# A hybrid of linear mixers and attention on one core: the first block's levels in PSUM pairs of their own, its third product in the product banks, and another order of the output product

## The chip, the cores and the metric

The kernel runs on one core of a Trainium2 chip. The metric is the device time of one execution in microseconds (us); lower is better.

## What is computed

The input x is 256 positions of 1024 numbers in float32. Two layers of a first block are followed by two layers of a second block; the change touches the first block only. In words of the reference, cut to what matters:

```python
def first_block(x, w_in, w_out, ...):
    for l in range(2):
        h = rms_norm(x, pre_mix_g[l])
        z = h @ w_in[l]                       # 1024 x 3256
        (a_q, a_f, a_i, a_g, b_q, b_k, b_v, b_code, b_g,
         c_q, c_kv, c_kr, d_q, d_k, d_v, d_beta, d_a, d_z) = split_columns(z)
        o_a = hgrn2_mixer(a_q, a_f, a_i, a_g, ...)
        o_b = gla_mixer(b_q, b_k, b_v, b_code, b_g, ...)
        o_c = mla_mixer(c_q, c_kv, c_kr, ...)
        o_d = gdn_mixer(d_q, d_k, d_v, d_beta, d_a, d_z, ...)
        mix = concatenate([o_a, o_b, o_c, o_d]) @ w_out[l]
        x = x + rms_norm(mix, post_mix_g[l])
        x = x + rms_norm(conv_glu_ffn(rms_norm(x, pre_ffn_g[l]), ...), post_ffn_g[l])
```

Each mixer gives 256 of the 1024 columns, in 4 heads of 64. a and b are gated linear attentions: for each pair of positions i >= j, the sum over the key's columns of q[i] k[j] exp(b[i] - b[j]), with b the running sum of the log gates, times v[j]. c is softmax attention with a low-rank query and key. d is the gated delta rule in chunks of 64, which needs the solution of a unit triangular system per chunk and head.

## The kernel before

**Products.** A weight comes from HBM in float32 (one DMA on the queue of SyncE, called SP below, per unit: L298) and is split on the chip into a high part by ScalarE (L308) and a low part by VectorE, now and then GpSimd (L311). A product of x and w is then three matmuls (`mm3`, L337 to L339: high x high, high x low, low x high), so the 48 matmuls of c's product (416 columns, two tiles of 128 positions, 8 blocks of the inner dimension) or the 96 of the output product (two tiles, two halves of 512 columns, 8 blocks of 128 rows of w_out) are counted with that three in them.

**PSUM.** Eight banks are four pairs, called acc, pd, pc and pa. A mixer's helper tiles come from `pt` (L198), which takes the mixer's pair from the table `BANKS` (L118). d has pd, c has pc, and a and b both have pa. Products without a bank of their own take the next of the rotation acc, acc, pa, pa (`acc`, L186); at c's product this rotation gives one bank of acc and one of pa. `first_banks` (L191) hands out both banks of a pair instead and moves the rotation on by the same two steps. The output product uses the banks of acc and pc.

**The mixers** (`first_layer`, L1293) are written as generators, planned in the order d, b, a, c. The levels of a and b are the function `gla` (L676). For each of 8 distances s it writes a decay table E (subtractions on VectorE, L711, and GpSimd, Exp on ScalarE), multiplies it with the queries on VectorE (L717, two rows per level) and with the keys on GpSimd (L721), takes eight matmuls into a bank of the mixer's pair (L735; L727 for the first level) and copies what the mask selects into the attention table A on VectorE (L744, two rows per level). L688 and L689 make the start of A, L752 and L753 apply it to the values, and `head_norm` (L581) with the transposes of L398 puts the result into mT, the input of the output product.

d's triangular system is solved in two parts. The 16 x 16 blocks on the diagonal go through DRAM (scr) into the tile d_Z and are inverted on VectorE by a recursion: seven pairs L1127, L1128, then L1130, L1131, L1132 and L1133, each needing the one before. The result goes out to DRAM (scv, L1134) and back as d_V (L1144). Then TensorE goes on, with steps on ScalarE and VectorE between: transposes (L1147), L1170, L1185, L1191, then the merging of blocks (L1162, L1178, L1191), and the recurrence over chunks (L1199 to L1233).

**What sets the order.** The program is written in the order of the generators, but each engine's order is made by the Tile framework's scheduler, which plays the program through a timeline of its own and starts what is ready. A bank, a buffer or a place in the plan of the weights (`ORDER1`, L28, is the order in which the eight blocks of w_out are loaded, split and multiplied; 0 and 1 are a's rows, 2 and 3 b's, 4 and 5 c's, 6 and 7 d's) therefore moves instructions on all engines. On the chip each engine runs its instructions in that order, one after the other, and waits where an input is not there yet.

Of the kernel before, what the change touches and what calls it, by code (L numbers as in the profile page):

```python
# [24 lines left out]
FF2 = 4096  # L25
EPS = 1e-6
NEG = -1e30
ORDER1 = (6, 7, 4, 5, 0, 1, 2, 3)  # L28
ORDER2 = (0, 1, 4, 5, 2, 3, 6, 7)
LEVELS = (32, 16, 8, 4, 2, 1)  # L30
WMAX = 1024
# [83 lines left out]
RUN2 = (0, 1, 0, 2, 1, 3, 0, 2, 3)  # L115
STAG = {"d": "d", "m": "d", "c": "c", "b": "c", "a": "a", "e": "e", "e2": "e"}

BANKS = {"m": ("pd", "pa"), "d": ("pd", "pd"), "c": ("pc", "pc"), "a": ("pa", "pa"), "b": ("pa", "pa"), "e": ("pa", "pa"), "e2": ("acc", "acc")}  # L118
NX = "N"
ACCS = ("acc", "acc", "pa", "pa")  # L120
NBANK = {"acc": 2, "pd": 2, "pc": 2, "pa": 2}
# [7 lines left out]
class K:  # L129
# [68 lines left out]
    def pt(self):  # L198
        self.turn = not self.turn
        return self.bank(BANKS[self.g][self.turn])  # L200

# [673 lines left out]
    def mixer_c(self, l, xT):  # L875
        nc, a = self.nc, self.a
# [8 lines left out]
        gn = self.z([128, 384], "c_gn")  # L885
        for ap, o, n in ((a["mla_q_norm_g"][l], 0, 256), (a["mla_kv_norm_g"][l], 256, 128)):
            nc.sync.dma_start(gn[:, o:o + n], bass.AP(tensor=ap.tensor, offset=ap.offset, ap=[[0, 128], [1, n]]))
        pz = self.tm(xT, (("c", l), 2, 416))
        kT = [self.z([96, 2, 256], "c_kT") for _ in range(2)]
        cT = [self.z([128, 256], "c_cT") for _ in range(3)]  # L890
        qT, V = [None] * 2, [None] * 2
# [345 lines left out]
    def plan_first(self, l, nxt):  # L1237
# [6 lines left out]
        for mixer in PLAN1:  # L1244
            for key, nk, c, n in blocks[mixer]:
                self.plan((key, l), w, D, nk, c, n)
        for kk in ORDER1:
            self.plan(("out", l, kk), a["w_out"][l, kk * 128:kk * 128 + 128], 128, 1, 0, D)
# [61 lines left out]
    def first_layer(self, l, last):  # L1310
# [9 lines left out]
        g2 = self.gains(a["post_mix_g"][l])  # L1320
        accs = self.big_out(self.mT, ("out", l), ORDER1)
        xT = self.norms((accs, g2, False), self.gains(a["pre_ffn_g"][l]))
# [455 lines left out]
```

## Time and profile before

| what | value |
|---|---|
| median of three runs | 1547.57 us (1544.92 to 1551.36) |
| the profiled execution's own time | 1551.53 us |
| its span on the core | 1549.4 us |
| mean granted clock of TensorE | 0.98 of full speed |
| TensorE busy | 1475.8 us, 95% |
| VectorE busy | 1002.3 us, 65% |
| ScalarE busy | 825.3 us, 53% |
| GpSimd busy | 280.1 us, 18% |
| DMA | 152 GB/s over the span |

The span is the time from the first instruction to the last on the core. The mixers of layer 0 lie at about 60 to 206 us of it, those of layer 1 at about 450 to 604; the rest are the FFNs and the second block. PE is TensorE, PEld its loading of weights, DVE VectorE, ACT ScalarE, POOL GpSimd, SP the queue of DMA issues. A matmul's time in the rows is longer than the distance to the next, since matmuls overlap in the pipeline.

### The profile page before, as it was taken

Reading aid. Unit: us, or ns where it says so; the run is one execution under the profiler, and the core shown is the slowest. Engines: PE = TensorE matmul, PEld = TensorE weight load, DVE = VectorE, ACT = ScalarE, POOL = GpSimd, SP = SyncE. Lnnn points to the kernel's source line nnn. Section 1 sums busy time; section 2 is a strip of 40 time slices with the busy share of each in tenths; the row PEclk is TensorE's granted clock in tenths of the full one; section 3 lists DMA queues with packets and bytes.
Section 4 is the critical chain, followed back from the end, with each engine's and each line's share of the span. In section 5 each row is a group of like instructions: output and inputs, shape, how many; then the busy total and the mean of one; then the engine's idle time right before and its main releaser. Section 6 shows DMA issues by size and latency. Waiting matters only on the chain.

```text
span 1549.4 us, 24775 instructions
## 1 busy us (share of the span) xinstructions
PE 1475.8 (95%) x9491; PEld 1319.9 (85%) x9491; DVE 1002.3 (65%) x1741; ACT 825.3 (53%) x1435; POOL 280.1 (18%) x360
## 2 busy tenths in 40 slices
PE   7988999999998899999999999999999999999998
PEld 6967789999896787999978888899977888899996
DVE  5896667656698665656576875554566695654455
ACT  5634456545565344544555674555554575555553
POOL 1453320000244232000033122000015231100010
PEclk9997999999999789999999999999999999999999
DMA  7532155656453223566646343556554543465563
GB/s 233 152 109 84 55 160 182 190 183 199 140 157 112 77 71 110 182 186 190 184 142 192 104 139 116 179 188 190 190 184 135 166 124 110 130 190 186 189 195 109
DMA packets 165379, 236.80 MB, mean 153 GB/s; under 512 B 16052, under 2 KB 127246, under 8 KB 165262
## 3 DMA queue, kind: packets, MB, share of 16 engines
q1 hardware_dynamic: 165262, 235.24, 49.1%
q8 instruction: 74, 1.21, 0.3%
q14 instruction: 43, 0.35, 0.1%
HBM read 232.45 MB, written 2.76 MB: 152 GB/s over the span
## 4 chain that ended last, share of the span: by engine, by line
PE 79%; DVE 11%; ACT 4%; DMA 4%; issue 1%; POOL 1%; SPq 0%; ACTq 0%; DVEq 0%
PE acc L337 7%; PE acc L338 7%; PE acc L339 7%; PE pa L337 7%; PE pa L339 7%; PE pa L338 7%; PE pc L337 5%; PE pc L339 5%; PE pc L338 5%; PE pd L339 4%; PE pd L338 4%; PE pd L337 4%; DVE wl L311 2%; DVE gl_r L717 2%; ACT wh L308 1%
## 5 line engine op out<-in xcount | busy, mean ns | idle before, releaser
L311 DVE TENSOR_TENSOR wl<-raw,wh 128x1024 fp32r<-128x1024 f32 (+4 forms) x424 | 484.3, 1151 | 364.0 <-ACT wh L308 362.8
L308 ACT ACTIVATE wh<-raw 128x1024 fp32r<-128x1024 f32 (+4 forms) x420 | 433.1, 1035 | 410.3 <-PE pd L338 100.1
L311 POOL TENSOR_TENSOR wl<-raw,wh 128x1024 fp32r<-128x1024 f32 (+1 forms) x26 | 61.6, 2370 | 641.9 <-ACT wh L308 641.6
L339 PE MATMUL pa<-xTh,wl 128*128 128x256 f32 x512 | 145.6, 284 | 0.0
L337 PE MATMUL pa<-xTh,wh 128*128 128x256 f32 x512 | 145.5, 284 | 0.0
L338 PE MATMUL pa<-xTl,wh 128*128 128x256 f32 x512 | 145.1, 283 | 0.0
L339 PE MATMUL pd<-xTh,wl 128*128 128x256 f32 x432 | 122.4, 283 | 0.5 <-DVE wl L311 0.5
L337 PE MATMUL pd<-xTh,wh 128*128 128x256 f32 x432 | 122.3, 283 | 0.0
L338 PE MATMUL pd<-xTl,wh 128*128 128x256 f32 x432 | 122.2, 283 | 0.0
L337 PEld LDWEIGHTS pa<-xTh,wh 128*128 128x128 f32 x512 | 98.2, 192 | 0.3
L338 PEld LDWEIGHTS pa<-xTl,wh 128*128 128x128 f32 x512 | 98.2, 192 | 0.3
L339 PEld LDWEIGHTS pa<-xTh,wl 128*128 128x128 f32 x512 | 98.1, 192 | 0.2
L337 PEld LDWEIGHTS pd<-xTh,wh 128*128 128x128 f32 x432 | 82.8, 192 | 0.9
L338 PEld LDWEIGHTS pd<-xTl,wh 128*128 128x128 f32 x432 | 82.8, 192 | 0.9
L339 PEld LDWEIGHTS pd<-xTh,wl 128*128 128x128 f32 x432 | 82.8, 192 | 0.8 <-DVE wl L311 0.8
L338 PE MATMUL acc<-wl,f_h 128*128 128x512 f32 x200 | 78.4, 392 | 0.0
L338 PE MATMUL pc<-wl,f_h 128*128 128x512 f32 x200 | 77.8, 389 | 0.0
L339 PE MATMUL pc<-wh,f_l 128*128 128x512 f32 x200 | 77.5, 389 | 0.0
L339 PE MATMUL acc<-wh,f_l 128*128 128x512 f32 x200 | 77.2, 389 | 0.0
L337 PE MATMUL acc<-wh,xTh 128*128 128x512 f32 (+4 forms) x200 | 71.3, 360 | 1.4 <-ACT xTh L494 1.1
L337 PE MATMUL pc<-wh,f_h 128*128 128x512 f32 x200 | 71.3, 389 | 0.0
L337 PE MATMUL acc<-wh,f_h 128*128 128x512 f32 x200 | 71.3, 392 | 0.0
(635 smaller groups left out, 3815.5 us busy)
## 6 DMA issues: line engine op xcount, KB each, us to landing
raw<-in_w_in_dram SPq DMA_DIRECT2D x84, 512.0 KB, 3.8
raw<-in_w_mlp_up_dram SPq DMA_DIRECT2D x64, 512.0 KB, 3.7
raw<-in_w_mlp_down_dram SPq DMA_DIRECT2D x64, 512.0 KB, 3.5
raw<-in_ffn_w_gate_dram SPq DMA_DIRECT2D x44, 512.0 KB, 3.6
raw<-in_ffn_w_up_dram SPq DMA_DIRECT2D x44, 512.0 KB, 3.5
raw<-in_ffn_w_down_dram SPq DMA_DIRECT2D x44, 512.0 KB, 3.6
raw<-in_w_out_dram SPq DMA_DIRECT2D x32, 512.0 KB, 3.6
raw<-in_w_ple_gate_dram SPq DMA_DIRECT2D x16, 512.0 KB, 3.4
```

The source lines that it names most:

```text
L308: nc.scalar.activation(h[:, p], raw[:, p], AF.Copy)
L311: e.tensor_tensor(l[:, p], raw[:, p], h[:, p].bitcast(F), OP.subtract)
L337: t.matmul(out, ah, bh, start=first, stop=False, skip_group_check=True)
L338: t.matmul(out, ah, bl, start=False, stop=False, skip_group_check=True)
L339: t.matmul(out, al, bh, start=False, stop=last, skip_group_check=True)
L717: nc.vector.tensor_tensor(R[:, j].rearrange("p h (b s) -> p h b s", s=s), ev[:, ft[j], :, 1][:, None].to_broadcast([128, 2, 128 // s, s]), ...
```

## The change

The diff is whole; it has three parts.

```diff
-ORDER1 = (6, 7, 4, 5, 0, 1, 2, 3)
+ORDER1 = (2, 3, 0, 1, 6, 7, 4, 5)
...
-BANKS = {"m": ("pd", "pa"), "d": ("pd", "pd"), "c": ("pc", "pc"), "a": ("pa", "pa"), "b": ("pa", "pa"), "e": ("pa", "pa"), "e2": ("acc", "acc")}
+BANKS = {"m": ("pd", "pa"), "d": ("pd", "pd"), "c": ("pc", "pc"), "a": ("pa", "pa"), "b": ("pc", "pc"), "e": ("pa", "pa"), "e2": ("acc", "acc")}
...
-        pz = self.tm(xT, (("c", l), 2, 416))
+        pz = self.tm(xT, (("c", l), 2, 416), outs=self.first_banks("acc"))
```

The blocks of w_out now come in the order b, a, d, c. Mixer b takes its helper tiles from the pair pc, which c uses too, and a keeps pa for itself. c's product goes into the two banks of acc. Nothing is computed in another way, and the number of instructions that compute stays as it was. Outside the mixer stages of the first block's two layers, the order of the engines is unchanged.

On VectorE the last steps of d's recursion in layer 0, from the sixth of the seven pairs on. Before:

```order
L1127 TENSOR_TENSOR d_tmp<-d_Z,d_Y 64x72
L1128 TENSOR_REDUCE d_Y<-d_tmp 64x2x6
L587 TENSOR_REDUCE hn_ssq<-hn_sq 128x4
L1127 TENSOR_TENSOR d_tmp<-d_Z,d_Y 64x98
L1128 TENSOR_REDUCE d_Y<-d_tmp 64x2x7
L1130 TENSOR_TENSOR d_tmp<-d_Y,d_Z 64x512
L1131 TENSOR_REDUCE d_U<-d_tmp 64x64
L590 TENSOR_TENSOR hn_y<-pa,rs 128x256
L1132 TENSOR_TENSOR d_tmp<-d_U,d_Y 64x512
L592 TENSOR_TENSOR hn_o<-hn_y,a_g 128x256
L1133 TENSOR_REDUCE d_Y<-d_tmp 64x8x8
```

With the change, the last four steps; both rows of the sixth and of the seventh pair stand ahead of these, with other rows between them:

```order
L717 TENSOR_TENSOR gl_r<-gl_e,gl_q 128x256 x2
L711 TENSOR_TENSOR gl_e<-a_b 128x256
L1130 TENSOR_TENSOR d_tmp<-d_Y,d_Z 64x512
L311 TENSOR_TENSOR wl<-raw,wh 128x1024
L587 TENSOR_REDUCE hn_ssq<-hn_sq 128x4
L1131 TENSOR_REDUCE d_U<-d_tmp 64x64
L717 TENSOR_TENSOR gl_r<-gl_e,gl_q 128x256 x2
L744 COPY_PREDICATED gl_a<-cu,pa 128x64x4 x2
L1132 TENSOR_TENSOR d_tmp<-d_U,d_Y 64x512
L590 TENSOR_TENSOR hn_y<-pc,rs 128x256
L744 COPY_PREDICATED gl_a<-cu,pa 128x128x2 x2
L1133 TENSOR_REDUCE d_Y<-d_tmp 64x8x8
```

The levels of a from the third on, which stood behind L1133 before, now stand between the steps of the recursion, all but the last two L744. In all, 34 rows newly stand ahead of L1133 in layer 0: seven L311, ten L717, ten L744, five L711 and two L689. In layer 1 they are these and two more L744, two L587, two L590, one L592 and one L401.

On TensorE around L1147, the first matmuls that need d_V, in layer 0. Before (three matmuls of c's product in a row are the three of one `mm3`):

```order
L753 MATMUL pa<-a_v,gl_a 128x64
L1147 MATMUL pd<-cf,d_V 128x128 x8
L1170 MATMUL pd<-d_T,d_MT 128x64 x8
L398 MATMUL pa<-cf,hn_o 128x128 x2
L337 MATMUL pa<-wh,xTh 128x416
L338 MATMUL pa<-wl,xTh 128x416
L339 MATMUL pa<-wh,xTl 128x416
L337 MATMUL pa<-wh,xTh 128x416
```

With the change:

```order
L753 MATMUL pc<-a_v,gl_a 128x64
L753 MATMUL pa<-a_v,gl_a 128x64 x4
L1147 MATMUL pd<-cf,d_V 128x128 x8
L1170 MATMUL pd<-d_T,d_MT 128x64 x4
L398 MATMUL pc<-cf,hn_o 128x128 x2
L1170 MATMUL pd<-d_T,d_MT 128x64 x4
L912 MATMUL pc<-cf,c_cn 128x128 x3
L913 MATMUL pc<-cf,c_cn 96x128
L337 MATMUL acc<-wh,mTh 128x512
L338 MATMUL acc<-wl,mTh 128x512
L339 MATMUL acc<-wh,mTl 128x512
```

Before, 30 of the 48 matmuls of c's product and all levels of a stood behind L1147; now c's product is complete and a's levels are done before it, and six matmuls of the output product (into acc) follow it. Of the output product's 96 matmuls, 18 stood ahead of d's last L398 and 78 behind it; now 27 stand between L1147 and d's last L1233, and 69 behind. In layer 1, nine stand ahead of L1147, 41 between and 46 behind.

On SP around d's store and loads in layer 0, before:

```order
L1122 DMA d_Z<-scr 64x16x16
L881 DMA c_wuq<-in_mla_w_uq_dram 128x384 x2
L884 DMA c_wkv<-in_mla_w_ukv_dram 128x512
L887 DMA c_gn<-in_mla_q_norm_g_dram 128x256
L887 DMA c_gn<-in_mla_kv_norm_g_dram 128x128
L1134 DMA scv<-d_Y 64x16x16
L1144 DMA d_V<-scv 128x4x128 x2
L298 DMA raw<-in_w_out_dram 128x1024 x6
```

With the change:

```order
L1122 DMA d_Z<-scr 64x16x16
L298 DMA raw<-in_w_out_dram 128x1024 x2
L881 DMA c_wuq<-in_mla_w_uq_dram 128x384
L298 DMA raw<-in_w_out_dram 128x1024
L881 DMA c_wuq<-in_mla_w_uq_dram 128x384
L884 DMA c_wkv<-in_mla_w_ukv_dram 128x512
L887 DMA c_gn<-in_mla_q_norm_g_dram 128x256
L887 DMA c_gn<-in_mla_kv_norm_g_dram 128x128
L298 DMA raw<-in_w_out_dram 128x1024
L298 DMA raw<-in_ffn_w_gate_dram 128x4x256
L1134 DMA scv<-d_Y 64x16x16
L1144 DMA d_V<-scv 128x4x128 x2
```

Before, two loads of w_out were ahead of the store of scv, and six and the first of the FFN behind it; now all eight and that one are ahead.

## Rows read from the trace of the kernel before

**Rows 1.** Stretch, its length, busy PE, PEld, DVE, ACT, POOL, clock, DMA share, GB/s
```profile
88.04:124.01 35.97, 24.84 (x130) 20.61 (x129) 29.79 (x77) 6.88 (x16) 14.11 (x26) 0.83 0.32 89
124.01:182.66 58.65, 55.55 (x422) 48.64 (x423) 38.18 (x84) 30.09 (x84) 19.73 (x36) 0.93 0.26 83
182.66:206.29 23.63, 23.63 (x120) 19.31 (x120) 12.23 (x24) 10.05 (x19) 8.31 (x7) 1.00 0.39 122
485.58:516.34 30.76, 17.19 (x89) 14.79 (x88) 24.94 (x65) 4.22 (x11) 11.19 (x20) 0.75 0.27 75
516.34:578.50 62.16, 58.55 (x422) 51.46 (x423) 39.28 (x90) 30.63 (x86) 20.18 (x37) 0.88 0.26 82
578.50:604.22 25.72, 25.62 (x120) 21.23 (x121) 12.58 (x25) 10.02 (x19) 8.31 (x7) 0.92 0.37 109
```

**Rows 2.** Busy time of VectorE to the recursion's end, layers 0 and 1
```profile
88.04:118.76 30.72, 28.94 (x75) 0.89 0.31 87
485.58:510.50 24.92, 23.45 (x62) 0.81 0.26 75
```

**Rows 3.** Timeline, layer 0: start, us, engine line op out<-in [idle before <-releaser]
```profile
118.09 0.67 DVE L1133 TENSOR_REDUCE d_Y<-d_tmp 64x64 f32<-64x512 f32 x1
...
118.84 0.59 SPq L1134 DMA_DIRECT2D scv<-d_Y  x1
...
124.01 1.11 PE L1147 MATMUL pd<-cf,d_V 128*128 128x128 f32 x4 [1.73 <-DMA d_V<-scv]
```

**Rows 4.** VectorE, 88 to 119: group xcount | busy us, mean ns | idle before
```profile
L717 DVE TENSOR_TENSOR gl_r<-gl_e,gl_q 128x256 f32<-128x256 f32 x22 | 10.2, 513 | 0.0
```

**Rows 5.** VectorE's groups from 130 to 206 us
```profile
L311 DVE TENSOR_TENSOR wl<-raw,wh 128x1024 fp32r<-128x1024 f32 x8 | 9.6, 1220 | 4.0 <-ACT wh L308 4.0
L717 DVE TENSOR_TENSOR gl_r<-gl_e,gl_q 128x256 f32<-128x256 f32 x10 | 7.4, 777 | 0.3 <-ACT gl_e L713 0.3
L744 DVE COPY_PREDICATED gl_a<-cu,pa 128x256 f32<-128x256 uint8 x12 | 5.6, 530 | 0.0
L711 DVE TENSOR_TENSOR gl_e<-a_b 128x256 f32<-128x256 f32 x5 | 2.1, 414 | 0.0
...
L689 DVE TENSOR_TENSOR gl_a<-pa,cf 128x512 f32<-128x512 f32 x2 | 1.4, 680 | 0.0
```

**Rows 6.** TensorE's groups of a's levels, 124 to 182.7 us
```profile
L735 PE MATMUL pa<-gl_r,gl_e 128*128 128x128 f32 x48 | 6.7, 283 | 2.2 <-DVE gl_a L744 2.2
...
L688 PE MATMUL pa<-gl_q,a_k 128*128 128x256 f32 x8 | 2.2, 379 | 0.0
```

**Rows 7.** Timeline of TensorE in c's product, layer 0
```profile
131.44 0.55 PE L339 MATMUL pa<-wh,xTl 128*128 128x416 f32 x1
131.79 0.55 PE L337 MATMUL pa<-wh,xTh 128*128 128x416 f32 x1
...
132.57 0.35 PE L337 MATMUL pa<-wh,xTh 128*128 128x416 f32 x1
132.76 0.35 PE L338 MATMUL pa<-wl,xTh 128*128 128x416 f32 x1
```

**Rows 8.** Timeline of TensorE, end of d's chain and output product, layer 0
```profile
182.05 0.39 PE L1232 MATMUL pd<-d_Sp,d_kT 128*128 128x64 f32 x2
182.27 0.39 PE L1233 MATMUL pd<-d_vn,d_AT 128*128 128x64 f32 x2
...
188.09 0.49 PE L337 MATMUL pc<-wh,mTh 128*128 128x512 f32 x1
...
205.90 0.39 PE L339 MATMUL pc<-wh,mTl 128*128 128x512 f32 x1
```

**Rows 9.** TensorE in two windows of 4 us: busy, granted clock, DMA share, GB/s
```profile
116.00:120.00 4.00, 1.69 (x9) 0.50 0.00 0
576.00:580.00 4.00, 4.00 (x21) 0.50 0.01 2
```

**Rows 10.** Timeline of TensorE, end of d's chain, layer 1
```profile
576.57 0.63 PE L1232 MATMUL pd<-d_Sp,d_kT 128*128 128x64 f32 x2
```

## Prediction

> **What bounds the kernel now.** I first read the page: TensorE is busy for 95% of the span, so time is won or lost only where it waits or runs at half clock. The change touches only the mixer stages of the two layers of the first block, so I cut these into three stretches and read the busy time by stretch [rows 1]. In layer 0, stretch one runs from 88.04 to 124.01 us (the levels of mixer b, and mixer d's recursion on VectorE), stretch two to 182.66 (d's chain on TensorE, with c's product, a's levels and c's attention between its steps), stretch three to 206.29 (the output product). Layer 1 has the same three. TensorE is busy for 24.84 of 35.97 us in stretch one, 55.55 of 58.65 in two and all of 23.63 in three; in layer 1 for 17.19 of 30.76, 58.55 of 62.16 and 25.62 of 25.72. So only stretch one has large holes.
>
> VectorE is the limit there: until the recursion's last row it is busy for 28.94 of 30.72 us [rows 2]. In order of time, that row (L1133) starts at 118.09, its result is stored at 118.84, and d's first matmul L1147, which needs it back as d_V, starts at 124.01 [rows 3]. Everything of d hangs on that row, and d's output ends the stage: its last L1233 starts at 182.27, the output product follows at 188.09, and its last row starts at 205.90 [rows 8].
>
> **The recursion comes later.** The pair pc for b lets a's levels run beside b's, and the order puts them between the recursion's steps on VectorE. Newly ahead of L1133 in layer 0 stand seven L311 of w_out, ten L717, ten L744, five L711 and two L689. Their prices are those that the same rows had later in the stage [rows 5]: 7 x 1.22 = 8.5; L717 7.4; L744 10 of 12, so 10/12 x 5.6 = 4.7; L711 2.1; L689 1.4; together 24.1 us. From that come off the 1.8 us that VectorE still idled there [rows 2], and the overlap of neighbours: 22 L717 of 0.513 us make 11.3, but 10.2 busy [rows 4], 0.05 each, for 34 rows 1.7. That leaves **20.6**. In layer 1 two more L744 (0.9) and six rows of the head norms of a and b, each taken as long as an L711, 0.42 (2.5) stand ahead too: 27.5, less 1.9 of overlap and 1.5 idle [rows 2], is **24.1**. So L1147 starts at about 144.5 instead of 124, and at 540.5 instead of 516.3. The ends of this term are 17.8 (ten L717 at 10.2/22 = 0.46, as the earlier ones ran, in place of 0.74) and 24.1 (nothing overlaps, no hole closes) in layer 0, 21.3 to 27.5 in layer 1.
>
> SP issues d's store now behind six more loads of w_out and one of the FFN. These wait for VectorE rows that stand ahead of L1133, so I cost them at nothing; if a load still occupied the engines the store would be late by what a load takes, at most 2 us, which I keep as an end.
>
> **What leaves the later stretches.** Stretches two and three took 82.3 us in layer 0 and 87.9 in layer 1. All the output product's 96 matmuls lie in them before and after in layer 0, so the order of w_out alone moves nothing into or out of them. Out of them go:
> - a's levels: 56 L735, of which 48 have 6.7 us, so 7.8 in all; eight L688 with 2.2 [rows 6]; four L727 of the same shape, 1.0. That is 11.0; a burst overlaps its neighbour of another group a little, and I take **10.5 us**.
> - 30 matmuls of c's product. At half clock they start 0.34 apart, at full clock 0.19 [rows 7]. By those rows the clock rose at about 132.2, so the first 8, from 129.56 on, ran at half: 8 x 0.345 + 22 x 0.19 = **6.9 us**. They now run ahead of the levels, where TensorE waits anyway.
>
> In layer 1 nine matmuls of the output product also come ahead of L1147 (9 x 0.233 = 2.1, from 78 in the 18.2 us between 188.09 and the end [rows 8]), and 12 small ones of a and b (0.11 each, since a pair follows the last pair by 0.22 [rows 8]: 1.3).
>
> Sum for layer 0: +20.6 - 10.5 - 6.9 = +3.2. Layer 1: +24.1 - 17.4 - 3.4 = +3.3. Together **+6.5 us**. So the two moves nearly cancel: the holes of stretch one are not closed, they are wider, and what fills them is what was already filling d's chain.
>
> Two terms I set against each other. Stretch two keeps about 38 us of TensorE work in place of 55.6, so more of d's steps are without cover; TensorE idled 3.1 us there before, and I bound the growth by 0 and 3 us per layer. Against it, in layer 1 the clock fell to half in the last part of the chain, 0.50 from 576 to 580 us though TensorE was fully busy [rows 9]; the chain's end ran so for about 10 us, which cost 5, and the work now lies differently, so it may not come back. I count both at nothing.
>
> **The clock.** From 116 to 120 us the granted clock was 0.50, the lower level (1.2 GHz), with TensorE busy for 1.69 of 4 us [rows 9]; it was back at full clock (2.4 GHz) only in c's product, at 132 [rows 7]. Stretch one is now 56 us long with the same thin matmuls, and stretch two begins with small ones and only six of the output product. The Trainium skill (TensorE: Matmul & The Clock Gate, What's actually happening) says that half rate is the default and activity releases it. By that rule d's chain begins at half clock and has little that would raise it, which speaks against this change: 1569 instead of 1554.1. The row at 116 agrees with it; the one at 576 (half clock at a fully busy engine) does not.
>
> **The rivals.**
> *Slower: d's chain runs at half clock.* A pair of small matmuls takes 0.63 us at half clock [rows 10] and 0.39 at full [rows 8], 1.6 times as much. Of the 38 us left in stretch two about 3 are output product, 35 small matmuls. If half of these run at half clock, that adds 35/2 x 0.6 = 10 us per layer, of which the chain's waits hide some 3: +7.5 each, +15 in all, so 1554.1 + 15 = 1569. It decides if the clock, once down, doesn't rise again between L1147 and the nine matmuls of the output product ahead of the last L1233. For it: a mean clock below 1 in all three stretches of layer 1 (0.75, 0.88, 0.92 [rows 1]). Against it: layer 0's stretch two ran at full clock after 132 with as many small matmuls.
>
> *Faster: VectorE runs its new queue unhindered and the clock holds.* The ten L717 that stood in the later stretch took 0.74 each [rows 5], the 22 earlier ones 0.46 [rows 4]; at that spacing each layer gains 2.8. The drop at 572 goes, -5.1. And c's dense product in front keeps the full clock until L1147 and its followers, which ran at half from 124.0 to 129.6: -2.8 per layer. Together 5.6 + 5.1 + 5.6 = 16.3: 1538. For it: the late L717 ran beside GpSimd's work of the same level, which an interleaved order may spread. Against it: GpSimd's rows for a move along with the L717, and c's product is over long before L1147.
>
> That the change doesn't do what it says is no rival here: the orders show both moves.
>
> **How the numbers follow.** Durations are of one execution, 1551.53 us, 4.0 above the median of the three runs; I add the sum to the median, 1547.57 + 6.5 = **1554.1**. A measurement of this kernel tells about 0.5% (7.7 us) from no change. The forecast's own range, with the ends of the first term, the waits and one clock drop more or less, is 1545 to 1561; chance 0.46. The slower rival has 0.32 (1561 to 1577), the faster 0.22 (1530 to 1541). Faster by over 0.5% (below 1539.8) is nearly all of the faster rival: 0.21. Slower (above 1555.3) is the slower rival and the upper end of the forecast's range, 0.08 of it: 0.40. Same is left with 0.39. To leave out no more than 2 in 10, the range goes from 1531 to 1572, half of each rival and a little more.
>
> **What would show it.** Right: L1133 ends near 139 and 534 us and L1147 starts near 144.5 and 540.5, the last L1233 near 190, and the stage ends 1 to 5 us later in each layer. TensorE's holes in stretch one are then longer than before, with waits for L744 and L717. Wrong by the slower rival: a granted clock of 0.5 in much of what follows L1147, pairs of 0.63 us. Wrong by the faster: L1147 by 136 us, L717 at 0.41 throughout, PEclk at 1.00 in stretch two. If L1133 ended before 125 us, the first step, VectorE's order as the limit, would be what failed.

## The result, and the profile after

The changed kernel takes **1555.89 us** (median of 7 runs, 1553.49 to 1558.09); the kernel before, on the same chip, 1545.95 (7 runs). The ratio is 1.0059, with a 95% interval of 1.0040 to 1.0078: slower by 9.9 us. The forecast was 1554.1, +6.5 us.

The profiled execution took 1553.49 us (span 1551.4), only 2.0 more than the profiled one of before (1551.53). Both belong to a spread that goes with the granted clock; more on this below, since most of the difference between the medians is there.

The same three stretches per layer as in [rows 1], begun where the same row of the program stands (0.84 us earlier in layer 0, 2.6 later in layer 1); columns as there:

```profile
87.20:141.54 54.34, 43.77 (x231) 38.58 (x230) 48.52 (x115) 18.23 (x35) 27.05 (x36) 0.82 0.40 124
141.54:191.34 49.80, 48.52 (x364) 40.92 (x365) 18.35 (x53) 19.97 (x67) 9.76 (x26) 0.89 0.07 23
191.34:207.80 16.46, 16.37 (x71) 12.77 (x71) 11.02 (x16) 8.61 (x15) 7.32 (x6) 1.00 0.58 178
488.20:541.40 53.20, 41.02 (x225) 37.03 (x223) 49.36 (x122) 18.26 (x42) 28.85 (x44) 0.81 0.35 107
541.40:591.00 49.60, 47.01 (x355) 39.82 (x354) 15.55 (x42) 21.32 (x61) 7.77 (x15) 0.93 0.18 55
591.00:602.90 11.90, 11.01 (x48) 8.59 (x48) 6.63 (x14) 4.30 (x11) 4.41 (x5) 1.00 0.44 140
```

Stretch one grew from 35.97 to 54.34 us and from 30.76 to 53.20; the other two together shrank from 82.28 to 66.26 and from 87.88 to 61.50. Layer 0 is 2.4 us longer, layer 1 3.9 shorter. TensorE's holes in stretch one are 10.6 and 12.2 us, where they were 11.1 and 13.6: c's product and a's levels fill what the delay adds and little more.

VectorE up to the end of the recursion's last row, as in [rows 2] (length, busy, clock, DMA):

```profile
87.20:134.74 47.54, 45.63 (x107) 0.86 0.41 130
488.20:532.08 43.88, 43.43 (x103) 0.87 0.37 116
```

In time (start, us, engine, line; as [rows 3]):

```profile
134.08 0.66 DVE L1133 TENSOR_REDUCE d_Y<-d_tmp 64x64 f32<-64x512 f32 x1
...
134.81 0.59 SPq L1134 DMA_DIRECT2D scv<-d_Y  x1
138.71 0.93 SPq L1144 DMA_DIRECT2D d_V<-scv  x2
...
141.54 0.69 PE L1147 MATMUL pd<-cf,d_V 128*128 128x128 f32 x2 [0.71 <-DMA d_V<-scv]
```

L1133 starts at 134.08 instead of 118.09, after 45.63 us of VectorE work in 47.54: the order that the change made on VectorE is the limit. Behind L1133 the way out and back is longer too: the loads of d_V are issued 3.90 us after the store, where before they came 2.50 us after it (store at 118.84, [rows 3]):

```profile
121.34 0.93 SPq L1144 DMA_DIRECT2D d_V<-scv  x2
```

In layer 1 L1133 starts at 531.41 (509.82 before) and the loads are issued by 535.6 and land 3.1 us later at most, but TensorE still has nine matmuls of the output product ahead of L1147, at half clock:

```profile
537.46 0.78 PE L337 MATMUL acc<-wh,mTh 128*128 128x512 f32 x1
...
541.40 1.03 PE L1147 MATMUL pd<-cf,d_V 128*128 128x128 f32 x8
```

VectorE's groups in layer 0's stretch to the end of L1133 (xcount | busy us, mean ns | idle), to be set beside [rows 4] and [rows 5]:

```profile
L717 DVE TENSOR_TENSOR gl_r<-gl_e,gl_q 128x256 f32<-128x256 f32 x31 | 14.0, 491 | 0.0
L311 DVE TENSOR_TENSOR wl<-raw,wh 128x1024 fp32r<-128x1024 f32 x6 | 7.3, 1211 | 0.3 <-ACT wh L308 0.3
...
L744 DVE COPY_PREDICATED gl_a<-cu,pa 128x256 f32<-128x256 uint8 x10 | 4.3, 480 | 0.0
```

31 L717 have 14.0 us, 0.45 each: the ten that came from the later stretch no longer take the 0.74 they took there.

The end of d's chain on TensorE, layer 0 (as [rows 8] and [rows 10]):

```profile
182.62 0.43 PE L1226 MATMUL pd<-d_vb,d_V 128*128 128x64 f32 x2
182.98 0.68 PE L1227 MATMUL pd<-d_S,d_wT 64*128 64x64 f32 x2
...
189.15 0.63 PE L339 MATMUL pc<-wh,mTl 128*128 128x512 f32 x1
189.58 0.42 PE L1233 MATMUL pd<-d_vn,d_AT 128*128 128x64 f32 x2
189.84 0.39 PE L1232 MATMUL pd<-d_Sp,d_kT 128*128 128x64 f32 x2
...
190.95 0.39 PE L1233 MATMUL pd<-d_vn,d_AT 128*128 128x64 f32 x2
```

Pairs go from 0.43 us to 0.68 as the clock falls at 182.9, though TensorE has no hole there, and back to 0.39 after nine matmuls of the output product.

### The profile page after: what moved, and what is told of

It is laid out like the page before. It is cut to its first block, busy times and chain, and to the rows that moved or that the text cites. A ratio compares the mean times of both kernels' runs of the same rounds, so it can differ in the third digit from the quotient of the medians.

```text
span 1551.4 us, 24787 instructions
## 1 busy us (share of the span) xinstructions
PE 1480.1 (95%) x9483; PEld 1324.0 (85%) x9491; DVE 994.9 (64%) x1741; ACT 824.5 (53%) x1435; POOL 291.8 (19%) x360
## 4 chain that ended last, share of the span: by engine, by line
PE 72%; DVE 14%; DMA 5%; ACT 4%; issue 3%; POOL 2%; SPq 0%; ACTq 0%; DVEq 0%; POOLq 0%
PE acc L339 6%; PE acc L337 6%; PE acc L338 6%; PE pa L338 6%; PE pa L337 6%; PE pa L339 6%; PE pc L337 5%; PE pc L339 5%; PE pc L338 5%; PE pd L339 4%; PE pd L338 4%; PE pd L337 4%; DVE wl L311 4%; ACT wh L308 1%; DVE gl_r L717 1%
## 5 line engine op out<-in xcount | busy, mean ns | idle before, releaser
L311 DVE TENSOR_TENSOR wl<-raw,wh 128x1024 fp32r<-128x1024 f32 (+4 forms) x424 | 484.3, 1150 | 348.2 <-ACT wh L308 347.6
L311 POOL TENSOR_TENSOR wl<-raw,wh 128x1024 fp32r<-128x1024 f32 (+1 forms) x26 | 62.4, 2403 | 638.3 <-ACT wh L308 599.2
L337 PE MATMUL acc<-wh,xTh 128*128 128x512 f32 (+4 forms) x216 | 76.3, 360 | 1.4 <-ACT xTh L494 1.1
L339 PE MATMUL acc<-wh,xTl 128*128 128x512 f32 (+4 forms) x216 | 76.5, 356 | 0.7 <-DVE xTl L496 0.7
L338 PE MATMUL acc<-wl,xTh 128*128 128x512 f32 (+4 forms) x216 | 75.8, 352 | 0.0
```

The lines of the kernel that those rows point to most:

```text
L311: e.tensor_tensor(l[:, p], raw[:, p], h[:, p].bitcast(F), OP.subtract)
L337: t.matmul(out, ah, bh, start=first, stop=False, skip_group_check=True)
L338: t.matmul(out, ah, bl, start=False, stop=False, skip_group_check=True)
L339: t.matmul(out, al, bh, start=False, stop=last, skip_group_check=True)
```

## The experiments

All are compared with runs of the kernel before on the same chip. In the table "clock" is the median over the executions of TensorE's mean granted clock, "L1147" the start of d's first matmul in layer 0, "stage" the time from d's first L1107 to the first matmul (L433) behind the output product in the profiled execution, for layers 0 and 1. "Profiled" is that execution's own time, and "half clock" its time at a granted clock of 0.50 from 60 to 240 and from 440 to 650 us, where the mixer stages lie. O is the new order of w_out, P c's product in the banks of acc, B the pair pc for b; the change is O + P + B.

| kernel | median us | ratio to before, interval | clock | L1147 | stage 0, 1 | profiled | half clock |
|---|---|---|---|---|---|---|---|
| before | 1546 to 1548 | | 0.983 | 124.0 | 117.6, 126.8 | 1551.53 | 54.6 |
| the change (O + P + B) | 1555.89 | 1.0059 (1.0040 to 1.0078) | 0.978 | 141.5 | 119.9, 121.7 | 1553.49 | 58.0 |
| O | 1549.04 | 1.0025 (1.0002 to 1.0048) | 0.982 | 123.4 | 118.2, 119.5 | 1546.66 | 41.0 |
| P | 1560.65 | 1.0081 (1.0056 to 1.0106) | 0.975 | 127.9 | 124.0, 128.0 | 1558.70 | 68.3 |
| B | 1566.26 | 1.0128 (1.0098 to 1.0158) | 0.972 | 134.4 | 127.4, 128.4 | 1567.08 | 81.9 |
| P + B | 1577.40 | 1.0187 (1.0154 to 1.0220) | 0.968 | 141.8 | 136.6, 134.2 | 1581.50 | 105.8 |
| O + P | 1554.33 | 1.0044 (1.0026 to 1.0063) | 0.977 | 129.1 | 118.0, 129.7 | 1556.04 | 64.9 |
| P + B, fillers | 1593.30 | 1.0298 (1.0258 to 1.0338) | 0.976 | 145.9 | 140.8, 140.9 | 1591.20 | 61.4 |
| O + P + B, a's levels behind | 1543.57 | 0.9974 (0.9957 to 0.9991) | 0.981 | 131.7 | 113.0, 120.1 | 1542.89 | 51.2 |
| O + B | 1546.08 | 0.9981 (0.9962 to 1.0000) | 0.982 | 136.7 | 116.2, 123.5 | 1550.03 | 54.6 |
| O + P + B, a's levels and conversions behind | 1543.85 | 0.9966 (0.9948 to 0.9984) | 0.981 | 128.4 | 117.2, 114.8 | 1544.48 | 47.8 |
| O + B, conversions behind | 1541.52 | 0.9953 (0.9933 to 0.9972) | 0.986 | 131.3 | 114.1, 115.5 | 1541.42 | 34.1 |
| before again | 1546.84 | 0.9986 (0.9971 to 1.0001) | 0.983 | 123.1 | 118.9, 126.6 | 1554.79 | 61.4 |
| the change again | 1555.28 | 1.0035 (1.0010 to 1.0059) | 0.978 | 142.3 | 120.4, 125.3 | 1557.80 | 61.4 |

**The order of w_out alone (O).**

```diff
-ORDER1 = (6, 7, 4, 5, 0, 1, 2, 3)
+ORDER1 = (2, 3, 0, 1, 6, 7, 4, 5)
```

> Only the order of w_out's blocks is changed; the table of pairs and c's product are as before. If the recursion's place on VectorE is what counts (theory one), this leaves the same rows ahead of L1133 as before: L1133 starts within 1 us of 118.1, L1147 near 124, and the time is that of before within 3 us (near 1546). If the order of the output product is itself a price (rival, order), the time is 5 us or more from before.

Measured: L1133 at 116.6 (1.5 us from 118.1, where 1 was expected), L1147 at 123.4, +2.7 us with an interval that just leaves out no change. Alone, the order is next to nothing.

**c's product alone (P).**

```diff
-        pz = self.tm(xT, (("c", l), 2, 416))
+        pz = self.tm(xT, (("c", l), 2, 416), outs=self.first_banks("acc"))
```

> Only c's product goes into both banks of acc. Its 48 matmuls then stand ahead of L1147, and six more L311 (1.22 us each, 7.3 us) ahead of L1133, but no level of a. Theory one: L1133 near 125 us, L1147 near 131, 30 matmuls (6.9 us) fewer behind it; the two cancel and the time is 1546 within 4. The rival on the clock (c's dense product missing in the middle leaves d's chain at half clock) expects half clock for 10 us or more behind L1147 in both layers and 1555 or more already here.

Measured: +14.3 us. Counted from d's first L1107, L1147 comes 5.2 us later in layer 0 and 6.7 in layer 1, and 30 matmuls fewer (6.9 us by the prediction) stand behind it in each; the delay alone would be paid for. TensorE from L1147 to the last L1233, and from there to the output product's end, for layer 0 and then layer 1 (length, busy, clock, DMA, GB/s):

```profile
127.90:185.36 57.46, 56.58 (x417) 0.86 0.09 30
185.36:211.50 26.14, 24.22 (x95) 0.87 0.42 127
528.21:586.01 57.80, 56.44 (x430) 0.92 0.07 22
586.01:610.60 24.59, 20.94 (x83) 0.86 0.44 132
```

With 30 of c's dense matmuls gone from it, layer 0's stretch is 57.46 us long against 58.65 [rows 1], at a clock of 0.86 against 0.93, and the next falls from 1.00 to 0.87 and has 1.9 us of holes. The rival on the clock is what was seen there. In layer 1 it is not: the two stretches are at half clock for about 16 us, no longer than before (18.6), they are 5.5 us shorter, and the stage is 1.2 us longer, as theory one has it.

**The pair of b alone (B), and both without the order (P + B).**

```diff
-BANKS = {"m": ("pd", "pa"), "d": ("pd", "pd"), "c": ("pc", "pc"), "a": ("pa", "pa"), "b": ("pa", "pa"), "e": ("pa", "pa"), "e2": ("acc", "acc")}
+BANKS = {"m": ("pd", "pa"), "d": ("pd", "pd"), "c": ("pc", "pc"), "a": ("pa", "pa"), "b": ("pc", "pc"), "e": ("pa", "pa"), "e2": ("acc", "acc")}
```

> Only the pair of b is changed to pc. Six L311, one or two L717, one L711 and two L689 more stand ahead of L1133 (about 11 us), c's 48 matmuls all ahead of L1147, a's levels still behind it. Theory one: L1133 near 128, L1147 near 134, the time 1546 to 1552. Rival on the clock: 1555 or more, with half clock behind L1147.

> Pair of b and c's product changed, the order of w_out as before. The same rows stand ahead of L1133 as in the full change (30 L717, 22 L744, 8 L311). Theory one: L1133 near 134 and 531, L1147 near 141 and 541 as in the full change, and 1552 to 1560. Rival, order: the time is that of before or less (1546), and the order of w_out is what costs.

Measured: +20 and +31 us. B has L1133 at 126.7 and L1147 at 134.4, as expected, but not theory one's time. Its second and third stretch of layer 0 run at 0.88 and 0.86, where they had 0.93 and 1.00 before:

```profile
134.36:191.13 56.77, 55.74 (x418) 0.88 0.06 20
191.13:215.40 24.27, 20.64 (x82) 0.86 0.46 129
```

P + B came out above both branches of its expectation. It has the same rows ahead of L1133 as the change, L1133 at 134.5 and L1147 at 141.8, as there. And yet it is 21.5 us slower than the change: given the two others, the order of w_out is worth 21.5 us. Its second stretch, third stretch and the second of layer 1:

```profile
141.81:199.80 57.99, 56.55 (x354) 0.74 0.07 20
199.80:224.90 25.10, 21.25 (x80) 0.80 0.44 131
560.62:608.90 48.28, 45.37 (x330) 0.85 0.09 26
```

57.99 us at a clock of 0.74 where the change has 49.80 at 0.89: 30 us at half clock instead of 11. The step to the output product, in time:

```profile
199.15 0.63 PE L1233 MATMUL pd<-d_vn,d_AT 128*128 128x64 f32 x2
203.17 0.66 PE L398 MATMUL pd<-cf,hn_o 128*128 128x128 f32 x2 [3.39 <-DVE hn_o L592]
204.31 0.79 PE L337 MATMUL pc<-wh,mTh 128*128 128x512 f32 x1 [0.47 <-ACT mTh L400]
```

Behind the last L1233 TensorE waits 3.39 us for d's head norm, and the dense matmuls that follow begin at half clock (0.63 us each, 0.39 in [rows 8]). With d's blocks of w_out first, only 18 matmuls of the output product lie ahead of the last L1233 and none cover that head norm; with b's and a's first, 27 lie ahead and 39 cover it.

**Order and product (O + P).**

```diff
-ORDER1 = (6, 7, 4, 5, 0, 1, 2, 3)
+ORDER1 = (2, 3, 0, 1, 6, 7, 4, 5)
...
-        pz = self.tm(xT, (("c", l), 2, 416))
+        pz = self.tm(xT, (("c", l), 2, 416), outs=self.first_banks("acc"))
```

> c's product in the banks of acc together with the new order of w_out; b keeps pa, a's levels stay behind L1133. Of the output product 18 matmuls (layer 0) and 30 (layer 1) then lie between L1147 and the last L1233. If what the product alone lost (14 us) is dense matmuls missing from d's chain, the order puts some back: 1546 to 1554, with less time at half clock behind L1147 than the product alone. If order and product simply add (the order alone cost 2.7 us): 1563.

Measured: 1554.33, just past the end of the first range: the order gives back 6 of the product's 14 us. In layer 0 the chain runs at 0.92; in layer 1, with 30 of the output product's matmuls in it, at 0.83 all the same, so their number alone does not hold the clock:

```profile
129.10:184.00 54.90, 54.20 (x413) 0.92 0.09 30
523.90:590.90 67.00, 65.63 (x443) 0.83 0.07 21
```

**Fillers in d's chain (P + B).** All nine places where d's chain from L1147 on takes a bank go through a helper that first fills it.

```diff
+    def dense_pt(self):
+        p = self.pt()
+        for _ in range(2):
+            self.nc.tensor.matmul(p, self.identb, self.cb[:, 0:512], start=True, stop=True)
+        return p
...
-        four = lambda: self.pt().rearrange("p (h i) -> p h i", h=4)
+        four = lambda: self.dense_pt().rearrange("p (h i) -> p h i", h=4)
...
-                p = self.pt()[:, :256].rearrange("p (h i) -> p h i", h=4)
+                p = self.dense_pt()[:, :256].rearrange("p (h i) -> p h i", h=4)
```

> The pair of b and c's product changed, the old order of w_out, and ahead of the matmuls of each step of d's chain two matmuls of constants, 128x512, into the bank that the step then overwrites: 48 per layer, some 10 us of added TensorE work per layer at full clock, no other instruction changed. If the loss of that version (31 us) is TensorE at half clock for want of dense matmuls, the half-clock time behind L1147 falls to under 10 us per layer and the time is the same or lower in spite of the added work: 1557 to 1577. If the loss is waits of the chain or of the output product for d, the clock hardly matters and the added work shows: 1580 to 1598.

Measured: 1593.3, 16 us slower than without them; the expectation of the clock's theory failed as a total. The two layers tell why (TensorE from L1147 to the last L1233):

```profile
145.90:205.50 59.60, 56.76 (x391) 0.90 0.06 19
558.20:619.10 60.90, 57.80 (x389) 0.87 0.07 21
```

and the fillers' own row in layer 0 (37 of them have records there; busy, mean ns):

```profile
L410 PE MATMUL pd<-cb 128*128 128x512 bf16 x37 | 12.9, 417 | 0.2 <-issue 0.2
```

In layer 0 they lifted the clock from 0.74 to 0.90, and at least 12.9 us of added work (the 37 with records) made the stretch 1.6 us longer. In layer 1 they did not (0.85 to 0.87), and it grew by 12.6 us, from 48.28 to 60.90. The half-clock time left in the two stretches, some 12 and 16 us, is over the 10 that the first branch asked for. So the half clock costs about what the theory says, where it goes; work that computes nothing is no cheap way to make it go, and does not always. The later start of L1147 in layer 0 (145.9 in place of 141.8) adds to the loss.

**a's levels behind the recursion (O + P + B).**

```diff
+                if g == "G" and lv >= 2:
+                    late.enter_context(self.tc.issue_after(self.dY.ins))
```

(dY is L1133; VectorE's rows of a's levels from the third on then queue behind it.)

> The full change, with VectorE's rows of a's levels from the third on queued behind L1133, as they stood before the change. L1133 then starts near 122 us instead of 134, L1147 near 129, and 20 of a's 56 L735 come behind L1147. If the later recursion costs what it is late (theory one without its second half), the time falls by 10 us per layer, to 1536. If the moved work cancels it, as the prediction's sum has it, the time stays at 1556 within 5. If dense matmuls and clock decide, it is 1556 or more, since the order of the output product keeps only 18 ahead of the last L1233 in layer 1 in place of 50.

Measured: 1543.57, 12 us faster than the change and faster than before. L1133 at 124.6, L1147 at 131.7; from d's first L1107 to L1147 it is 11 us shorter in layer 0 and 15 in layer 1. Stage 0 is 6.9 us shorter, stage 1 1.6 (5.2 against the second profile of the change). That is about half of what the delay alone would give, and not what the prediction's sum had (no change); none of the three branches was met. The clock in the second stretches is 0.97 and 0.84:

```profile
131.70:185.80 54.10, 51.15 (x413) 0.97 0.10 29
521.20:575.90 54.70, 53.73 (x401) 0.84 0.09 24
```

**Pair and order (O + B).**

```diff
-ORDER1 = (6, 7, 4, 5, 0, 1, 2, 3)
+ORDER1 = (2, 3, 0, 1, 6, 7, 4, 5)
...
-BANKS = {"m": ("pd", "pa"), "d": ("pd", "pd"), "c": ("pc", "pc"), "a": ("pa", "pa"), "b": ("pa", "pa"), "e": ("pa", "pa"), "e2": ("acc", "acc")}
+BANKS = {"m": ("pd", "pa"), "d": ("pd", "pd"), "c": ("pc", "pc"), "a": ("pa", "pa"), "b": ("pc", "pc"), "e": ("pa", "pa"), "e2": ("acc", "acc")}
```

> The pair of b and the new order of w_out, c's product by the rotation. Of the output product 27 matmuls in layer 0 and 18 in layer 1 stand ahead of d's last L1233. Dense matmuls and clock: better than the pairs alone (1566), 1550 to 1560, with the gain in layer 0. If order and pairs simply add: 1569.

Measured: 1546.08, as before the change and below the range expected; 20 us better than B alone. The gain is in both layers (stages 11.2 and 4.9 us shorter), though only layer 0 has more matmuls of the output product in the chain. The clock there is 0.97, in layer 1 0.87:

```profile
136.70:189.40 52.70, 51.78 (x422) 0.97 0.08 22
526.60:582.20 55.60, 54.66 (x409) 0.87 0.09 23
```

Of the three parts it is the product's banks that make the change slower than this: +10 us. That they do it by letting a's levels in ahead of L1133 fits the run before, where the levels are put back behind it and the time is 1543.57.

**w_out's conversions behind the recursion too.**

```diff
+        if key[0] == "out":
+            stack.enter_context(self.tc.issue_after(self.dY.ins))
```

> As the run with a's levels behind the recursion, and VectorE's conversions of w_out (L311) queued behind L1133 too: 2 instead of 7 or 8 of them stand ahead of it, some 6 us less. L1133 starts near 118.5 and L1147 near 125.5 in layer 0. If every microsecond of the recursion's delay counts: 12 us less, 1532. If about half of it does, as the run before showed (10 us earlier, 12 us less in two layers): 1537. If what is left is TensorE's own work and clock: 1543 as before it.

> The pair of b and the new order, c's product by the rotation, w_out's conversions queued behind L1133: six fewer L311 ahead of it, L1133 near 122 instead of 129, and 36 of the output product's matmuls ahead of the last L1233 in layer 0. About half of the delay counts: 1539; nothing of it counts: 1546.

Measured: on top of a's levels behind, nothing (1543.85): the recursion ends 3 us earlier in layer 0, not 6, and the second stretch is 4 us longer at a lower clock, 0.85 instead of 0.97. (L1147 to the last L1233, both layers:)

```profile
128.40:186.70 58.30, 56.50 (x427) 0.85 0.20 67
519.20:573.80 54.60, 52.35 (x412) 0.88 0.23 68
```

On O + B: **1541.52**, 4.6 us better, between the two branches, and 0.47% below before. It is the lowest median, but its interval overlaps those of O + B and of the two kernels with a's levels behind. Second and third stretch of layer 0, second of layer 1:

```profile
131.30:187.60 56.30, 54.32 (x438) 0.98 0.15 48
187.60:203.50 15.90, 14.23 (x63) 1.00 0.72 207
517.50:572.20 54.70, 51.81 (x416) 0.94 0.21 60
```

This version keeps the clock best (0.986 over the program, 34.1 us at half clock in the stages); between d's first L1106 and L1133 stand two L311 in place of seven.

**Before and the change once more.**

> The kernel before, unchanged, for a second profile. 1546 within 3. If the half clock at the end of d's chain in layer 1 (10 us at 572) belonged to the one profiled execution, it is gone here and the stage of layer 1 is about 5 us shorter; if it belongs to the kernel, it is there again.

> The changed kernel, unchanged, for a second profile. 1556 within 3. L1133 near 134 and 531, L1147 near 141.5 and 541 again; where the clock falls may differ by several us per layer.

Measured: medians 1546.84 and 1555.28. The second profile of before again has the half clock at the end of d's chain (0.93 in the last of the two rows, [rows 9] shows it in the first profile):

```profile
518.00:580.10 62.10, 58.37 (x421) 0.88 0.27 82
580.10:605.50 25.40, 25.31 (x121) 0.93 0.37 114
```

But both profiled executions of before lie at the upper end of its runs, 1551.53 and 1554.79 us, with mean clocks of 0.980 and 0.977; whether an execution near the median has that drop too is not shown. The 80 executions of before that were timed with these experiments (one more, of 2892 us, is left out) go with their clock: 39 with at least 0.984 have a median of 1545.8 us, 15 with at most 0.980 one of 1553.0 (a mean clock of 0.985 and 0.979, so 1.1 us for each 0.001). The change's 11 executions all lie between 0.975 and 0.982, with a median of 1555.9; the 8 of before from 0.977 to 0.979 have 1553.4. So at like clock the change is 2.5 us slower, and the pairs of profiles say the same: 2.0 us (1553.49 and 1551.53) and 3.0 (1557.80 and 1554.79). Against the 26 executions of before that were timed beside it (median 1548.4), the second timing of the change is 6.9 us slower, not 9.9. Second profile of the change, second stretches:

```profile
142.30:192.00 49.70, 48.41 (x364) 0.90 0.08 23
542.60:595.20 52.60, 50.00 (x355) 0.87 0.18 53
```

## Why the prediction was right, and where it was not

**The recursion's delay: right in kind, VectorE's part of it too large.** Forecast +20.6 and +24.1 us for stretch one, measured +18.4 and +22.4. VectorE's rows stood where the order put them, and its queue was the limit. But counted from the stretch's start L1133 comes only 16.8 and 19.0 us later, below the term's lower ends (17.8 and 21.3): the ten late L717 ran like the early ones (0.45 us). The other 1.5 and 3.5 us come behind L1133, where the sum had nothing. In layer 0 it is the longer way from the store to the loads; the prediction kept up to 2 us for a late store, but the store was in time and the loads were late, and why is not shown. In layer 1 it is the nine matmuls of the output product, which the sum had as free ahead of L1147; they ran at half clock and held it up. The prediction expected TensorE's holes in stretch one to grow; they shrank by 0.6 and 1.4 us.

**What leaves the later stretches: right in layer 0, too small in layer 1.** Forecast -17.4 and -20.8, measured -16.0 and -26.4. The extra 5.6 us of layer 1 is clock: the two stretches had 18.6 us at half clock before and have 6.8 now, worth 5.9. The prediction named that drop and its price (5) and counted it at nothing. The two stretches also shared the work in another way than it said: stretch two kept 48.5 us of TensorE work in layer 0, not 38, and stretch three fell from 23.63 to 16.46 us (71 matmul records instead of 120). The idle time behind L1147, for which it allowed 0 to 3 us more, fell from 3.1 to 1.4 us.

**The sum: near in size by luck.** In the profiles the two layers together are 1.6 us shorter, not 6.5 longer: the sum was 8.1 us too high. It had each stage end 1 to 5 us later; layer 0's is 2.3 us longer and layer 1's 5.1 shorter. The whole execution is 2.0 longer; the 3.6 us between lie outside these stretches, most of them behind layer 1's, where VectorE's, ScalarE's and SP's orders are unchanged. And the medians lie 9.9 apart, 7.9 more than the profiled executions. Two steps failed, then, in opposite directions: the sum itself, chiefly the half clock of layer 1 counted at nothing, and the last step, to add a sum made against one execution to the median of the runs. That execution had a clock of 0.980, the median one of the 80 has 0.983. Of the 9.9 us between the medians, 2.5 remain at like clock; the other 7.4 (1553.4 less 1545.95) go with the clock. The moved work does cancel, roughly, as forecast, and what is left is that every execution of the changed kernel has as much half clock as only some of before have.

**The clock.** The rival on it was given 0.32 and 1569 us. It is what happened to P (in layer 0), B and P + B, and to P + B beyond its price (1577). That the change escaped most of it is the work of the order of w_out, of which the prediction said that it "moves nothing into or out of" the later stretches. True, and beside the point: it moves dense matmuls within them, from behind the chain into it, and this was worth 21.5 us once c's product and a's levels had left. The filler run shows the price in one layer directly (at least 12.9 us of work for 1.6 us of time as the clock rose).

The table's last two columns show how far the clock goes. In the profiles pairs of small matmuls start 0.43 us apart at half clock and 0.22 at full. If all work behaves so, half of the difference in half-clock time is what the clock costs, as an estimate. Against the profile of before it gives +1.7 us for the change (measured +2.0), -6.8 for O (-4.9), +6.8 for P (+7.2), +13.7 for B (+15.5), +25.6 for P + B (+30.0), +5.2 for O + P (+4.5) and 0 for O + B (-1.5); for O + B with the conversions behind, -10.2 (-10.1); for the second profiles, +3.4 for before (+3.3) and +3.4 for the change (+6.3). So between the profiles of all the combinations of the three parts, the clock makes nearly the whole difference, and delay and moved work cancel within a few us in each. The most that is left is 4.4 us in P + B, where TensorE also waits 3.4 us for d's head norm in each layer.

**The faster rival** asked for L1147 by 136 us and a clock of 1.00 in stretch two; it came at 141.5, at 0.89.

**What the sum hid.** That moved work and delay cancel holds for the combinations of the three parts, not for every order: with a's levels put back behind L1133 the same change gained 12 us, where the sum had 0. In layer 0 stretch one is 11 us shorter and stretch two, with 49 more matmul records in it, only 4.3 us longer (54.10 for 49.80): its clock was 0.97 instead of 0.89, while its holes grew from 1.3 to 3.0 us. Over the profiled executions (10.6 us apart) the clock accounts for 3.4 us by the estimate above; the other 7 are not clock.

What stays open is what decides where the clock falls: the chain of layer 1 ran at 0.83 with 30 of the output product's matmuls in it (O + P) and, in the change with 41, at 0.93 in one profile and 0.87 in the other.

## What to carry to other kernels

Where several small changes come together, time them in all combinations before giving each a price: here the parts cost +2.7, +14 and +20 us alone and +9.9 together, and the kernel with the lowest median leaves one of them out. When dense matmuls are moved out of a chain of small ones, ask what keeps TensorE's clock up there; order the product so that its blocks that are ready early can run inside the chain. And before adding a sum to a median, compare the profiled execution's clock with those of the other runs.

## What the runs showed that was not expected

A fully busy TensorE can be at half clock: 4.00 of 4.00 us busy at 0.50 [rows 9], and pairs of 0.68 us from 182.98 on in the changed kernel with only 0.3 us of holes in the 7 us before them; in each case the work was small matmuls, and full clock came back during dense ones. The time of an execution of before goes with its mean clock, by some 1.1 us for each 0.001, and so does most of its run-to-run spread of 1542 to 1557 us. And an order that alone makes next to no difference (1.0025) can be worth 21.5 us beside other changes.
